# A hybrid SSM and attention block: four q/k slabs go into Strassen pairs, and the SSM projection's products move

## The chip, the cores and the metric

The kernel runs on one core of a Trainium2 chip. A core has five engines that run their own instruction streams side by side: TensorE (PE; its weight loads are listed as PEld), VectorE (DVE), ScalarE (ACT), GpSimd (POOL) and SyncE (SP). In this kernel SP issues every DMA. Work in progress lies in SBUF and, for matmul results, in PSUM (eight banks of 128 x 512 float32). What is measured is the device time of one execution in microseconds (us).

## The reference

One decoder layer with sequence length 1024 and model width 1024, in float32, for batch 1:

```python
h = _rmsnorm(x, norm_w) * (1.0 + scale[:, None, :]) + shift[:, None, :]
proj = jnp.einsum("bsd,de->bse", h, w_in)
z_ssm, xbc, dt_raw, q, k, v, z_att, f_logit, g_logit = jnp.split(proj, offsets, axis=-1)
y_ssm = _ssd_branch(z_ssm, xbc, dt_raw, ...)     # Mamba-2, 16 heads of 64, chunks of 128
y_att = _fox_branch(q, k, v, z_att, f_logit, b_f)   # causal attention, 8 heads of 128
g_ssm, g_att = jnp.split(jax.nn.sigmoid(g_logit + b_gate), N_BRANCHES, axis=-1)
merged = g_ssm * (y_ssm @ w_proj_ssm) + g_att * (y_att @ w_proj_att)
x = x + gate[:, None, :] * (merged @ w_out)
return _rmsnorm(x, final_norm_w)
```

(The last lines are written with @ for the einsum of the reference.) `scale`, `shift` and `gate` come from c. Nearly all of the work is in matrix products: the input projection to 8472 columns, the scores and the weighted sums of attention, and the three projections of 1024 x 1024 at the end.

## The kernel before

**Numbers.** Each float32 operand is split into a high part (cast to fp32r, on ACT) and a low part (the rest, by a subtraction on DVE); a product is high x high + high x low + low x high, so three matmuls for one. The helper `split` (L97 to L99) does this. Nearly all cast and subtraction rows in the profile are its lines L98 and L99, whatever they work on.

**Stages, in order.** (1) h is normalized, transposed and kept in SBUF as eight blocks `hh` and `hl` (pool `hpool`); 64 KB of each partition. (2) The slabs of the input projection. A slab is 128 output columns over all 1024 positions. A plain slab (`c_slab`) takes 2 x 8 x 3 = 48 matmuls of 128 x 128 x 512 (L111 to L113). Two slabs can be made together as a pair (`c_pair`) by the Strassen-Winograd scheme: seven products of 12 matmuls (L497 to L500), so 84 for two slabs, with four sums of weights, seven splits and three additions of results on DVE. The list `PAIRS` names 19 pairs, made one after the other in the pool `pa`; the tuple `WPREP` hangs the sums of later weights on some of them. Results that are needed later are written to DRAM. (3) The Mamba scan (pools `sd`), with the v slabs and seven plain q/k slabs (`SPILL`) put between its steps; these are written to DRAM. (4) Attention, by head. (5) The projections `ps` (SSM), `pa` (attention) and `o` (output), each a 1024 x 1024 x 1024 product by the same seven-product scheme on blocks of 512.

**Attention.** `attend(h, ...)` works through four groups qq = 3, 2, 1, 0 of two blocks of 128 queries: score matmuls (tile `lg`, L1030), the masked addition with row minimum on DVE (L1031), the exponential on ACT (L1036), the scaling on POOL (L1039), transposes on PE (tile `tp`, L1051), the split (`pth`, `ptl`, L1054 and L1055), and the weighted sum (tile `pv`, L1061), which DVE multiplies by the gate (L1064). A head's output is stored by L1065. `qk_slab(h + 1)` gets the next head's q and k: a slab in `SPILL` is loaded from DRAM and split as a whole (two operations of 1024 columns); any other is made there as a plain slab from `hh` and `hl`, with its result split out of PSUM. q and k of a head have two buffers each. In the kernel before, nine slabs are made this way: q1, k1, q2, q3, k3, q4, q5, q6, k7.

**What sets the order.** The program is traced in Python order, and a scheduler then orders each engine's instructions by readiness and priority. The attention heads get a higher priority (`high_priority(offset=APRI)`); the slabs and the early products are placed where the heads leave room. Tiles come from pools with a fixed number of buffers per tag; an instruction that needs a buffer waits until it is free. `issue_after(ins)` orders the instructions of its block on the engine of `ins` behind `ins`, on that engine alone.

**The SSM projection's products.** The scheme's products are numbered 1 to 7. Products 1 and 2 use unchanged blocks of the right operand; 6, 7 and 4 use forms that DVE makes by subtractions; 5 uses b11 after a subtraction; 3 uses b22. Some need results of others: 6 adds product 1's copy (x1), 7 is accumulated onto 6 (its copy is u3), 5 adds x1 or u2 and u3, 4 belongs onto u3, and 3 onto 5. When h's memory is closed (`hctx.close()`, at head `HCLOSE`), the pool `fin` takes its place, and with it eight buffers for forms (`bh`, `bl`), the copies and the blocks b12 and b22. `early(js)` loads pieces of the right operand (`us_scr`), makes the forms and runs the products of `js` in the three PSUM banks of the tile `mm`, while attention still runs. In the kernel before, products 1 and 2 are traced at head 6 and product 6 at head 7; 7, 5, 4 and 3 follow behind the heads, in the main part (`prod_c`), which opens five more PSUM banks and the tiles of the pool `frp` when attention's memory is free.

Lines that matter: L44 to L60 (the tables), `prod_c` L906 to L916, `early` L933 to L972, `qk_slab` L977, `attend` L1011, the head loop L1072 to L1088, the main part L1091 to L1118.

Of the kernel before, what the change touches and what calls it, by code (L numbers as in the profile page):

```python
# [31 lines left out]
P = 128  # L32
# [14 lines left out]
PSPILL = ()  # L47
SB = (3, 4, 3)
HCLOSE = 6
EARLY = {6: (1, 2), 7: (6,)}  # L50
# [15 lines left out]
def build(ctx, tc, t):  # L66
# [807 lines left out]
    def post(i, p, ps, x, held, done):  # L874

        if i == 1:
            x[p] = fin_tile("x1", 4)
            A.copy(out=x[p], in_=ps)  # L880
            held[1, p] = ps
        elif i == 6:
            V.tensor_tensor(out=ps, in0=ps, in1=x[p], op=ALU.add)
            A.copy(out=x[p], in_=ps)
            held[6, p] = ps
        elif i == 7:
            if (6, p) not in held:
                V.tensor_tensor(out=ps, in0=ps, in1=x[p], op=ALU.add)
                held[6, p] = ps
            held["u3", p] = fin_tile("u3", 4)  # L890
            A.copy(out=held["u3", p], in_=ps)
        elif i == 5:
            u3 = held.pop(("u3", p))
            V.tensor_tensor(out=u3, in0=ps, in1=u3, op=ALU.add)
            V.tensor_tensor(out=ps, in0=ps, in1=x[p], op=ALU.add)
            held[5, p] = ps
            done(1, 1, p, u3)
        else:
            done(*RESULT[i], p, ps)
# [31 lines left out]
    sx, held = {}, {}  # L931

    def early(js):  # L933
# [6 lines left out]
        def form(i):  # L940
            fs = []
            for k in range(4):
                if i == 2:
                    e = piece(4 + k, LO)
                else:
                    e = piece(k, LO)
                    for q in {1: (), 6: (12, 22)}[i]:
                        V.tensor_tensor(out=e, in0=ub[q][k], in1=e, op=ALU.subtract)
                fs.append(b_split(e))
# [8 lines left out]
        if js == (6,):  # L958
            for p in range(4):
                hi, lo = w_in("ps", 6, p)  # L960
                ps = bank()
                for k in range(4):
                    c = slice(k * P, (k + 1) * P)
                    PE.matmul(ps, lhsT=hi[:, c], rhs=fs[6][k][0], start=(k == 0), stop=False)
                    PE.matmul(ps, lhsT=hi[:, c], rhs=fs[6][k][1], start=False, stop=False)
                    PE.matmul(ps, lhsT=lo[:, c], rhs=fs[6][k][0], start=False, stop=(k == 3))
                V.tensor_tensor(out=sx[p], in0=ps, in1=sx[p], op=ALU.add)
            return
        for p in range(4):
            mine = {}  # L970
            for i in js:
                prod_c(i, "ps", fs[i], sx, mine, done, p)  # L972

    with tc.tile_pool(name="at", bufs=1, side="right") as at, \
# [36 lines left out]
        def attend(h, q, vhl, zg):  # L1011
# [5 lines left out]
            for qq in (3, 2, 1, 0):  # L1017
# [25 lines left out]
                for jp in range(qq + 1):  # L1043
# [12 lines left out]
                    for kb in (2 * jp, 2 * jp + 1):  # L1056
# [3 lines left out]
                        for i, (x, y) in enumerate(((vh, pth), (vl, pth), (vh, ptl))):  # L1060
                            PE.matmul(pv[:, o0:256], lhsT=x[kb // 4][:, kb % 4, vs], rhs=y[:, d:d + m],  # L1061
                                      start=(kb == 0 and i == 0), stop=(kb == 2 * qq + 1 and i == 2))
# [9 lines left out]
        for h in range(AH):  # L1072
# [14 lines left out]
            for _ in range(PREP[h]):  # L1087
                u_scaled(next(prep))  # L1088

# [5 lines left out]
    with tc.tile_pool(name="finp", bufs=1, space=PSUM) as fpp_:  # L1095
        fpp.append(fpp_)


        done_early = sum(EARLY.values(), ())
        b = {**ub, **b_quads(us_scr, (11, 21))}  # L1100
# [3 lines left out]
        prep_u = True  # L1104
        for i in ORDER:
            if i in done_early:
                continue
            if i in (5, 4) and prep_u:
                prep_u = False
                for p in range(4):  # L1110
                    t2 = tt_tile()
                    V.tensor_tensor(out=b[11][p], in0=b[12][p], in1=b[11][p], op=ALU.subtract)
                    V.tensor_tensor(out=t2, in0=b[22][p], in1=b[11][p], op=ALU.subtract)
                    V.tensor_tensor(out=b[21][p], in0=b[21][p], in1=t2, op=ALU.subtract)
            prod_c(i, "ps", b_form(i, b, lambda: raw_tile()[:, :512]), sx, held, ssm_done)
# [134 lines left out]
```

## Time and profile before

| | us |
|---|---|
| median of 3 runs | 1224.31 (1223.64 to 1227.98) |
| the profiled execution's own time | 1224.89 |
| its span, first to last instruction | 1223.2 |
| PE busy | 1162.6 |
| PE weight loads busy | 976.3 |
| DVE busy | 957.2 |
| ACT busy | 626.5 |
| POOL busy | 88.3 |

The profile is one execution on the chip. In its time line a row gives start, duration, engine, line of the program, operation, the tile written and those read, and in brackets the idle time before it with what ended it. In the table of stretches a row gives the stretch and its length, then for each engine the busy time and the number of instructions, then the granted clock of PE (1.00 is full), the mean busy share of the 16 DMA engines, and GB/s; such a table can also be asked for one tile alone. A matmul's end is modelled and matmuls overlap, so the busy time of PE is an upper bound of its work.

### The profile page before, as it was taken

How to read it: one execution, taken by the hardware profiler on the slowest of the kernel's cores; microseconds unless marked ns; L12 is line 12 of the kernel's file. 1: busy time of each engine (PE TensorE's matmuls, PEld its weight loads, DVE VectorE, ACT ScalarE, POOL GpSimd, SP SyncE). 2: the span in 40 equal slices, each digit the busy share in tenths (PEclk: the TensorE clock that was granted, in tenths of full speed). 3: DMA queues.
4: the chain of work that ended last, by engine and by line, in shares of the span. 5: the costliest groups of instructions: out<-in, count | busy, mean ns of one | idle time of the engine just before them, and what ended most of it. 6: DMA issues, size and time to landing. Idle time of an engine off the chain costs nothing.

```text
span 1223.2 us, 18391 instructions
## 1 busy us (share of the span) xinstructions
PE 1162.6 (95%) x6206; PEld 976.3 (80%) x6206; DVE 957.2 (78%) x1950; ACT 626.5 (51%) x1252; POOL 88.3 (7%) x152
## 2 busy tenths in 40 slices
PE   4899999999999999999999989999989998999997
PEld 2788888788877878998987777888877886788876
DVE  6956689788987685589999986664677968989967
ACT  5554444453443334777676633454456644354465
POOL 2000000000000000000000002222322220000001
PEclk9899999999999999999999999999999999999999
DMA  8765543655485665646545658422255526965333
GB/s 351 274 233 184 185 154 93 231 189 189 129 309 167 224 224 200 202 152 223 187 150 186 199 213 294 155 92 73 87 176 195 182 77 239 326 190 182 104 96 147
DMA packets 109018, 228.26 MB, mean 187 GB/s; under 512 B 12362, under 2 KB 20220, under 8 KB 107900
## 3 DMA queue, kind: packets, MB, share of 16 engines
q1 hardware_dynamic: 108924, 227.09, 55.1%
q8 instruction: 49, 0.80, 0.3%
q14 instruction: 45, 0.37, 0.1%
HBM read 159.14 MB, written 67.90 MB: 186 GB/s over the span
## 4 chain that ended last, share of the span: by engine, by line
PE 66%; DVE 15%; DMA 12%; issue 4%; ACT 3%; POOL 1%; SPq 0%; DVEq 0%; POOLq 0%; ACTq 0%
PE pp L497 4%; PE pp L499 4%; PE pp L500 4%; PE pv L1061 4%; PE mm L497 3%; PE mm L499 3%; PE mm L112 3%; PE mm L500 3%; PE mm L113 3%; PE lg L1030 3%; PE mm L111 3%; DMA ab<-a_scr 3%; PE tp L1051 2%; PE mm L915 2%; PE mm L913 2%
## 5 line engine op out<-in xcount | busy, mean ns | idle before, releaser
L98 ACT CAST wh<-wr 128x512 fp32r<-128x512 f32 (+1 forms) x214 | 130.8, 619 | 171.7 <-DMA wr<-w_c 35.0
L99 DVE TENSOR_TENSOR wl<-wr,wh 128x512 fp32r<-128x512 f32 (+1 forms) x214 | 145.5, 686 | 44.9 <-ACT wh L98 44.6
L112 PE MATMUL mm<-hl,wh 128*128 128x512 f32 x288 | 116.4, 404 | 1.9 <-DVE hl L306 1.9
L111 PE MATMUL mm<-hh,wh 128*128 128x512 f32 x288 | 115.7, 406 | 0.1
L113 PE MATMUL mm<-hh,wl 128*128 128x512 f32 x288 | 115.1, 400 | 0.0
L136 PE MATMUL mm<-wh,hh 128*128 128x256 f32 (+1 forms) x256 | 73.8, 289 | 2.4 <-DVE tmp L348 2.4
L137 PE MATMUL mm<-wl,hh 128*128 128x256 f32 (+1 forms) x256 | 74.4, 292 | 0.0
L138 PE MATMUL mm<-wh,hl 128*128 128x256 f32 (+1 forms) x256 | 73.6, 288 | 0.0
L1036 ACT ACTIVATE pr<-pr,sm 128x1024 f32<-128x1024 f32 (+3 forms) x64 | 49.9, 780 | 44.8 <-DVE sm L1035 38.1
L1054 ACT CAST pth<-tp 128x512 fp32r<-128x512 f32 (+1 forms) x80 | 42.5, 542 | 53.5 <-PE tp L1051 43.7
L1031 DVE CUSTOM_DVE_ANT_0 pr<-lg,fb 128x512 f32<-128x512 f32 (+1 forms) x96 | 51.3, 551 | 18.7 <-PE lg L1030 13.2
L112 PEld LDWEIGHTS mm<-hl,wh 128*128 128x128 f32 x288 | 55.0, 191 | 13.2 <-DVE hl L306 3.3
L113 PEld LDWEIGHTS mm<-hh,wl 128*128 128x128 f32 x288 | 54.9, 191 | 10.3
L111 PEld LDWEIGHTS mm<-hh,wh 128*128 128x128 f32 x288 | 54.5, 191 | 10.5 <-ACT hh L305 0.7
L690 ACT ACTIVATE ab<-ab,acs 128x128 f32<-128x128 f32 x128 | 41.2, 391 | 37.7 <-DMA ab<-a_scr 34.1
L1055 DVE TENSOR_TENSOR ptl<-tp,pth 128x512 fp32r<-128x512 f32 (+1 forms) x80 | 49.9, 630 | 10.2 <-ACT pth L1054 9.8
L1039 POOL TENSOR_SCALAR pr<-pr,sm 128x1024 f32<-128x1024 f32 (+3 forms) x64 | 52.2, 816 | 78.2 <-DVE sm L1038 65.4
L98 ACT CAST sh<-sr 128x512 fp32r<-128x512 f32 x57 | 33.9, 619 | 42.3 <-DVE sr L479 31.3
L796 POOL TENSOR_TENSOR fl<-fl,mhalf 128x8 f32<-128x8 f32 x1 | 1.6, 1648 | 699.0 <-DVE fl L794 699.0
L136 PEld LDWEIGHTS mm<-wh,hh 128*128 128x128 f32 x256 | 48.8, 191 | 2.8 <-DVE tmp L348 2.6
L138 PEld LDWEIGHTS mm<-wh,hl 128*128 128x128 f32 x256 | 49.1, 192 | 0.0
L137 PEld LDWEIGHTS mm<-wl,hh 128*128 128x128 f32 x256 | 48.9, 191 | 0.2
(406 smaller groups left out, 3485.5 us busy)
## 6 DMA issues: line engine op xcount, KB each, us to landing
wr<-w_c SPq DMA_DIRECT2D x116, 256.0 KB, 3.7
wa<-w_ada SPq DMA_DIRECT2D x8, 1024.0 KB, 11.4
g_scr<-gt SPq DMA_DIRECT2D x16, 512.0 KB, 4.2
ab<-a_scr SPq DMA_DIRECT2D x32, 256.0 KB, 3.9
gt<-g_scr SPq DMA_DIRECT2D x32, 256.0 KB, 4.0
wr<-w_ps SPq DMA_DIRECT2D x28, 256.0 KB, 2.7
wr<-w_pa SPq DMA_DIRECT2D x28, 256.0 KB, 2.7
wr<-so SPq DMA_DIRECT2D x28, 256.0 KB, 2.7
```

Of the source, the lines that this page charges most:

```text
L98: A.copy(out=hi[:, :n], in_=raw[:, :n])
L99: eng.tensor_tensor(out=lo[:, :n], in0=raw[:, :n], in1=f32(hi[:, :n]), op=ALU.subtract)
L111: PE.matmul(ps, lhsT=hi[:, cs], rhs=xh[k][:, hs], start=(k == 0), stop=False)
L112: PE.matmul(ps, lhsT=hi[:, cs], rhs=xl[k][:, hs], start=False, stop=False)
L113: PE.matmul(ps, lhsT=lo[:, cs], rhs=xh[k][:, hs], start=False, stop=(k == 7))
L136: PE.matmul(o, lhsT=xh[k][:, ts], rhs=hi[:, cs], start=(k == 0), stop=False)
L137: PE.matmul(o, lhsT=xh[k][:, ts], rhs=lo[:, cs], start=False, stop=False)
L138: PE.matmul(o, lhsT=xl[k][:, ts], rhs=hi[:, cs], start=False, stop=(k == 7))
L497: PE.matmul(ps, lhsT=f[0][:, w], rhs=xh[:, hs], start=(first and k == 0), stop=False, skip_group_check=True)
L499: PE.matmul(ps, lhsT=f[0][:, w], rhs=xl[:, hs], start=False, stop=False, skip_group_check=True)
L500: PE.matmul(ps, lhsT=f[1][:, w], rhs=xh[:, hs], start=False, stop=(k == 3), skip_group_check=True)
L1039: G.tensor_scalar(out=pr[:, :n], in0=pr[:, :n], scalar1=sm[:, 1:2], scalar2=0.5, op0=ALU.mult, op1=ALU.mult)
```

## The change

Four of the nine plain slabs that are made during attention (q4, q5, q6 and k7) are made as two Strassen pairs, (q4, q5) and (q6, k7), ahead of the last two pairs of gates in the pair stage. They are written to DRAM and loaded by `qk_slab` like those of `SPILL`. The last slab made from h is then k3, and h's memory is closed at head 3 (6 before). Products 1 and 2 are traced at head 3 (6 before), products 6 and 7 together at head 5 (6 at head 7, 7 in the main part before). Product 4 is traced behind the head loop, its matmuls on PE ordered behind the last matmul of the last head's weighted sum (`pv`); it used the open bank of product 6 before and gets a bank of its own now, with u3 added by DVE. Its form is made from pieces again (three subtractions for each block). The main part keeps products 5 and 3, and loads b11 alone (b11 and b21 before). The special form of `early` for product 6 alone is gone. The results of products 2 and 4 wait in DRAM (`m_scr`) until the main part loads them; before, it was product 2's alone.

```diff
--- before.py
+++ after.py
@@ -44,10 +44,10 @@
 Z0, XB0, Q0, K0, ZA0, G0 = 0, 8, 18, 26, 34, 42
 FIRST = (G0, G0 + 1, G0 + 2)
 SPILL = (("q", 0), ("k", 0), ("k", 2), ("k", 4), ("q", 7), ("k", 5), ("k", 6), )
-PSPILL = ()
+PSPILL = (("q", 4), ("q", 5), ("q", 6), ("k", 7))
 SB = (3, 4, 3)
-HCLOSE = 6
-EARLY = {6: (1, 2), 7: (6,)}
+HCLOSE = 3
+EARLY = {3: (1, 2), 5: (6, 7)}
 ORDER = (1, 2, 6, 7, 5, 4, 3)
 WPREP = {1: [('ps', 0)], 2: [('ps', 1)], 3: [('ps', 2)], 6: [('ps', 3), ('pa', 0)], 8: [('pa', 1)], 10: [('pa', 2), ('g', 0)], 12: [('pa', 3), ('g', 2), ('g', 3)], 11: [('g', 1)], 13: [('G', 0)], 15: [('o', 0)], 16: [('o', 1)], 17: [('o', 2)], 18: [('o', 3)]}
 PREP = (6, 1, 0, 0, 0, 0, 0, 0, 1)
@@ -896,6 +896,8 @@
             held[5, p] = ps
             done(1, 1, p, u3)
         else:
+            if i == 4 and (6, p) not in held:
+                V.tensor_tensor(out=ps, in0=ps, in1=held["u3", p], op=ALU.add)
             done(*RESULT[i], p, ps)
 
     def prod_bank(i, p, held):
@@ -928,7 +930,7 @@
         SP.dma_start(out=gt, in_=g_scr[j][:, HI if tk else LO])
         return gt
 
-    sx, held = {}, {}
+    sx, held, last_mm = {}, {}, {}
 
     def early(js):
 
@@ -942,10 +944,16 @@
             for k in range(4):
                 if i == 2:
                     e = piece(4 + k, LO)
+                elif i == 7:
+                    e = raw_tile()[:, :512]
+                    V.tensor_tensor(out=e, in0=ub[22][k], in1=ub[12][k], op=ALU.subtract)
                 else:
                     e = piece(k, LO)
-                    for q in {1: (), 6: (12, 22)}[i]:
+                    for q in {1: (), 6: (12, 22), 4: (12, 22)}[i]:
                         V.tensor_tensor(out=e, in0=ub[q][k], in1=e, op=ALU.subtract)
+                    if i == 4:
+                        e2 = piece(4 + k, LO)
+                        V.tensor_tensor(out=e, in0=e2, in1=e, op=ALU.subtract)
                 fs.append(b_split(e))
             return fs
 
@@ -955,21 +963,12 @@
             m_scr[ch, tk, p] = dram.tile([P, 512], F32, name=f"m_scr{ch}{tk}{p}")
             SP.dma_start(out=m_scr[ch, tk, p], in_=gt)
         fs = {i: form(i) for i in js}
-        if js == (6,):
-            for p in range(4):
-                hi, lo = w_in("ps", 6, p)
-                ps = bank()
-                for k in range(4):
-                    c = slice(k * P, (k + 1) * P)
-                    PE.matmul(ps, lhsT=hi[:, c], rhs=fs[6][k][0], start=(k == 0), stop=False)
-                    PE.matmul(ps, lhsT=hi[:, c], rhs=fs[6][k][1], start=False, stop=False)
-                    PE.matmul(ps, lhsT=lo[:, c], rhs=fs[6][k][0], start=False, stop=(k == 3))
-                V.tensor_tensor(out=sx[p], in0=ps, in1=sx[p], op=ALU.add)
-            return
         for p in range(4):
-            mine = {}
+            mine = {("u3", p): held["u3", p]} if js == (4,) else {}
             for i in js:
                 prod_c(i, "ps", fs[i], sx, mine, done, p)
+            if 7 in js:
+                held["u3", p] = mine["u3", p]
 
     with tc.tile_pool(name="at", bufs=1, side="right") as at, \
             tc.tile_pool(name="atp", bufs=1, space=PSUM) as atp:
@@ -1058,8 +1057,9 @@
                         o0 = 128 if (last and kb % 2) else 0
                         m = 256 - o0
                         for i, (x, y) in enumerate(((vh, pth), (vl, pth), (vh, ptl))):
-                            PE.matmul(pv[:, o0:256], lhsT=x[kb // 4][:, kb % 4, vs], rhs=y[:, d:d + m],
-                                      start=(kb == 0 and i == 0), stop=(kb == 2 * qq + 1 and i == 2))
+                            last_mm["pv"] = PE.matmul(pv[:, o0:256], lhsT=x[kb // 4][:, kb % 4, vs],
+                                                      rhs=y[:, d:d + m], start=(kb == 0 and i == 0),
+                                                      stop=(kb == 2 * qq + 1 and i == 2))
                 o = zg[:, qq * 256:(qq + 1) * 256]
                 V.tensor_tensor(out=o, in0=pv[:, :256], in1=o, op=ALU.mult)
             SP.dma_start(out=o_scr[h], in_=zg[:, :S])
@@ -1086,6 +1086,8 @@
                     ub = b_quads(us_scr, (12, 22))
             for _ in range(PREP[h]):
                 u_scaled(next(prep))
+        with tc.issue_after(last_mm["pv"].ins):
+            early((4,))
 
 
     frp = rctx.enter_context(tc.tile_pool(name="frp", bufs=1, side="right"))
@@ -1096,23 +1098,15 @@
         fpp.append(fpp_)
 
 
-        done_early = sum(EARLY.values(), ())
-        b = {**ub, **b_quads(us_scr, (11, 21))}
+        b = {**ub, **b_quads(us_scr, (11,))}
+
         def ssm_done(ch, tk, p, ps):
             V.scalar_tensor_tensor(out=mq[11 + 10 * ch + tk][p], in0=g_in(p + 4 * ch, tk), scalar=1.0, in1=ps,
                                    op0=ALU.add, op1=ALU.mult)
-        prep_u = True
-        for i in ORDER:
-            if i in done_early:
-                continue
-            if i in (5, 4) and prep_u:
-                prep_u = False
-                for p in range(4):
-                    t2 = tt_tile()
-                    V.tensor_tensor(out=b[11][p], in0=b[12][p], in1=b[11][p], op=ALU.subtract)
-                    V.tensor_tensor(out=t2, in0=b[22][p], in1=b[11][p], op=ALU.subtract)
-                    V.tensor_tensor(out=b[21][p], in0=b[21][p], in1=t2, op=ALU.subtract)
-            prod_c(i, "ps", b_form(i, b, lambda: raw_tile()[:, :512]), sx, held, ssm_done)
+        for p in range(4):
+            V.tensor_tensor(out=b[11][p], in0=b[12][p], in1=b[11][p], op=ALU.subtract)
+        for i in (5, 3):
+            prod_c(i, "ps", b_form(i, b), sx, held, ssm_done)
 
         for ch, tk, p in m_scr:
             SP.dma_start(out=mq[11 + 10 * ch + tk][p], in_=m_scr[ch, tk, p])
```

## The prediction

> **What bounds the kernel now.** I read the page first, then the busy time by stage, then the time line and the chain of waits around the attention heads and behind them.
>
> ```profile
> span 1223.2 us, 18391 instructions
> ...
> PE 1162.6 (95%) x6206; PEld 976.3 (80%) x6206; DVE 957.2 (78%) x1950; ACT 626.5 (51%) x1252; POOL 88.3 (7%) x152
> ...
> PE   4899999999999999999999989999989998999997
> PEclk9899999999999999999999999999999999999999
> ```
>
> PE is the engine that sets the end nearly everywhere. But a matmul's end is modelled, so the row of nines hides short idle times. The step from one 512-column matmul to the next shows what one really costs:
>
> ```profile
> 1018.94 0.39 PE L915 MATMUL pp<-bh,wl 128*128 128x512 f32 x1
> 1019.17 0.39 PE L913 MATMUL pp<-bh,wh 128*128 128x512 f32 x1
> ...
> 1025.76 1.28 DVE L1112 TENSOR_TENSOR b<-b,b 128x512 f32<-128x512 f32 x2
> ```
>
> So 0.23 us per matmul, not 0.39, and for DVE 1.28 - 0.68 = 0.60 us per 512-column operation in a row, 0.68 alone. By stage (the pairs; attention from the end of k3's slab, where the change begins to differ; the two stretches behind attention):
>
> ```profile
> core 0: us, PE busy (x) PEld busy (x) DVE busy (x) ACT busy (x) POOL busy (x), PEclk, DMA share, GB/s
> 123.00:500.00 377.00, 372.44 (x1642) 301.71 (x1641) 295.02 (x457) 165.37 (x284) 0.00 (x0) 1.00 0.58 194
> ...
> 808.00:1018.40 210.40, 200.65 (x1178) 174.16 (x1176) 144.30 (x381) 108.59 (x221) 56.02 (x94) 0.98 0.38 124
> 1018.40:1060.00 41.60, 38.83 (x162) 29.96 (x163) 37.98 (x63) 18.08 (x32) 0.00 (x0) 1.00 0.95 337
> 1060.00:1136.00 76.00, 76.00 (x330) 61.80 (x329) 68.32 (x113) 38.18 (x68) 0.00 (x0) 1.00 0.64 204
> ```
>
> In the pairs 377.0 / 1642 = 0.23: PE has no room. From 1060 on it is the same (76.0 / 330). Between 1018.4 and 1060, 162 x 0.23 = 37.3 of 41.6 us: 4.3 idle. In attention the q/k slabs and the early SSM products ("fillers" from here on; all of them write the tile mm) run in what the heads leave of PE. A head ends where its output is stored; the windows below are cut at these stores, and the PE count is the number of fillers in each.
>
> ```profile
> 887.34 0.32 SPq L1065 DMA_DIRECT2D o_scr<-zg  x1
> ...
> 1018.81 0.38 SPq L1065 DMA_DIRECT2D o_scr<-zg  x1
> ```
>
> ```profile
> 808.00:819.70 11.70, 7.95 (x32) 5.40 (x30) 0.68 (x1) 0.58 (x1) 1.00 0.22 69
> 819.70:858.50 38.80, 22.59 (x89) 16.14 (x89) 1.28 (x2) 1.11 (x2) 1.00 0.25 88
> 858.50:887.30 28.80, 12.18 (x48) 8.73 (x48) 1.36 (x2) 1.09 (x2) 1.00 0.28 92
> 887.30:917.00 29.70, 6.37 (x24) 4.29 (x24) 1.36 (x2) 1.09 (x2) 0.99 0.52 176
> 917.00:960.10 43.10, 21.46 (x84) 15.19 (x84) 3.39 (x5) 3.42 (x6) 0.93 0.55 178
> 960.10:998.30 38.20, 24.09 (x96) 17.67 (x96) 5.51 (x8) 1.77 (x3) 1.00 0.47 146
> 998.30:1018.80 20.50, 0.00 (x0) 0.00 (x0) 0.00 (x0) 0.00 (x0) 1.00 0.12 40
> ```
>
> Take the fillers' 0.23 us each off, and a head costs net: rest of head 1: 11.7 - 7.4 = 4.3; head 2: 18.3; head 3: 17.8; head 4: 24.2; head 5: 23.8; head 6: 16.1; head 7: 20.5. Together 125.0 and 373 x 0.23 = 85.8 of fillers: 210.8. Heads 2, 3 and 6 have fillers enough and PE is full. Head 4 runs out of them, head 5 begins where h's memory turns into the memory of the early products, and head 7 has none. What the turn of the memory costs shows in the time line, the windows and the chain of waits:
>
> ```profile
> 915.89 0.69 DVE L99 TENSOR_TENSOR bl<-wr,bh 128x512 fp32r<-128x512 f32 x1 [1.42 <-ACT bh L98]
> ...
> 918.25 0.80 PE L1030 MATMUL lg<-kh,qh 128*128 128x512 f32 x1 [3.17 <-DVE sm L1031]
> ```
>
> ```profile
> 914.90:918.20 3.30, 0.18 (x2) 0.03 (x1) 2.31 (x7) 2.53 (x5) 0.00 (x0) 0.71 1.06 406
> 918.20:922.20 4.00, 3.95 (x14) 3.53 (x14) 2.06 (x8) 3.02 (x7) 3.85 (x4) 0.50 1.00 354
> ```
>
> ```profile
> 909.50 5.72 DMA wr<-us_scr
> ...
> 930.24 2.44 DMA wr<-us_scr
> ```
>
> The forms of products 1 and 2 stand in DVE's queue, wait for ACT's cast and that for a piece landing 5.7 us after its issue; the head's own DVE work stands behind them, PE waits 3.2 us, and in the windows the granted clock is 0.50 for the next 4.0 us, another 2.0 lost.
>
> **The change, part by part.** *Four slabs (q4, q5, q6, k7) leave attention:* 4 x 48 matmuls, 192 x 0.23 = 44.2 us of fillers. *Two pairs come into the pair stage:* 2 x 84 = 168 matmuls; PE is full there, so all of it lies on the path: +38.6. Their DVE work (14 operations of 0.60, 8.4 us in a pair of 19.3) hides beside PE, since DVE has 82 us free of 377; with that cover gone it would be up to 17. *Four more stores and four reloads* of 512 KB go through SP's queue. The stores lie in the pair stage (DMA share 0.58), the reloads in attention (0.38): nothing by themselves. A reloaded slab also needs a split:
>
> ```profile
> L99 DVE TENSOR_TENSOR kl<-qt,kh 128x1024 fp32r<-128x1024 f32 x4 | 4.9, 1218 | 1.8 <-ACT kh L98 1.8
> ```
>
> 1.2 us on DVE in place of four operations of 0.60 (two of the weights, two of the result). *Product 7 moves into head 5's early call, product 4 behind the last pv matmul.* Attention before held 96 + 48 + 36 of products 1, 2, 6 and 7; the 12 left of product 7 ran behind it. After, it holds 192: products 1, 2, 6, 7. So attention from 808 loses 373 - 192 = 181 fillers, 41.6 us. DVE there: -16 x 0.60 (slabs) + 4.9 (reloads) - 1.8 (three adds of product 7 that accumulating in one bank saves) + 12 (16 form operations of product 4 and its four weight halves, which the order on PE doesn't hold back) = +5.5: 150 us.
>
> *h's memory is freed at head 3.* The last slab that reads h is then k3, done at 808, not k7 at 907. The turn described above comes 100 us earlier, and the SSM's forms with it: 8 + 4 piece loads, then 8 for product 4, on SP behind the reloads.
>
> What do the heads cost with 192 fillers? Those run as soon as they are ready, so I let heads 2 and 3 be filled (18.3 and 17.8, as now) and the rest to be short. For an unfilled head the trace gives 17.8 from below (a filled one: all its waits covered) and 24.2 from above (head 4, half filled and without cover in its second half); head 7, the only one with none at all, took 20.5, which includes an end behind which nothing follows. I take 20.0 for heads 4 to 6, 20.5 for head 7. For the turn: heads 4 and 5 were 24.2 + 23.8 - 2 x 17.8 = 12.4 over filled ones; half of it I put to want of fillers, half, 6.2, to the turn (its bounds: 0, if the waiting heads 2 and 3 cover it, and 12.4). Sum: 4.3 + 18.3 + 17.8 + 60.0 + 20.5 + 6.2 + 44.2 = 171.3, against 210.8: -39.5.
>
> *The passage.* Behind attention PE had 12 matmuls of product 7, and then waited for b11's load, DVE's subtraction, ACT's cast:
>
> ```profile
> 1020.56 0.69 DVE L1112 TENSOR_TENSOR b<-b,b 128x512 f32<-128x512 f32 x1 [2.24 <-DMA b<-us_scr]
> ...
> 1022.03 1.19 PE L913 MATMUL pp<-bh,wh 128*128 128x512 f32 x4 [0.62 <-ACT bh L98]
> ```
>
> After, product 4 gives 48 matmuls, 11.0 us, in the three mm banks that stay open, and b11 can land meanwhile. The order that holds them behind the last pv matmul holds nothing else: what stands behind them on PE are products 5 and 3, which need b11 and the memory of attention anyway. Behind attention are 48 x 3 = 144 matmuls of the SSM, not 156: -2.8. Of the 4.3 us idle I take 2.7 back (bounds: 0 and 4.3), as DVE loses eight subtractions there and gains four adds (product 4 needs product 7's sum): -5.5 in all. b21's four loads go where DMA is full (0.95); four more reloads of finished parts come when it has eased (0.64 from 1060 on): nothing.
>
> Total: 38.6 - 39.5 - 5.5 = -6.4. The profiled execution took 1224.9 (1.7 outside its span), so 1218.5; the runs' median is 0.6 lower: **1217.9, said as 1218.0**. It is about what 24 matmuls cost (5.5): the idle time stays nearly what it was.
>
> [...]
>
> **The rivals.**
> (a) *The heads stay covered.* The early products spread over heads 3 to 7, and each costs 17.8: 4 x 17.8 = 71.2 in place of 80.5, so -9.3: 1208.6. For it: heads 2, 3 and 6 were full with 48 to 96 fillers, and 192 over five heads are 38 each. Against: only eight operand tiles exist for forms, and fillers run when they can.
> (b) *Attention starves, slower than before.* The fillers are gone by head 4 and heads 4 to 7 each cost what head 4 did: 4 x 24.2 = 96.8, so +16.3: 1234. The gain is gone from 80.5 / 4 + 6.4 / 4 = 21.7 us a head on. For it: DVE rises from 144 of 210 us to 150 of 171, and sits in every head's chain. Against: head 7.
> (c) *Product 4 comes late.* Its forms are not ready at the last pv matmul: a piece's landing (2.4 to 5.7), three subtractions, a cast and a split (3.0) lie open, about 7, the half clock costs 2.0 more, and the 2.7 are not won: +11.7, 1229.6.
> (d) *Half clock in the heads.* Two idle stretches like that at 914.9 in each of heads 4 to 7: 17.8 + 2 x (3.3 + 2.0) = 28.4 a head, +33: 1251. Against: head 7 had a clock of 1.00. [...]
> That the change doesn't do what it says (early products that start no sooner) would leave the 192 fillers to later heads; that is (a).
>
> **How the numbers follow.** The forecast, with its own range 1212 to 1226, gets 0.54; (a) 0.18, (b) 0.14, (c) 0.10, (d) 0.04. 0.5% is 6.1 us, about what a measurement of this kernel can tell from no change: faster is below 1218.2, slower above 1230.4. A little over half of the forecast's chance is faster: 0.28, with (a) 0.46. Slower are (b), (d) and a little of (c): 0.19. The rest is 0.35. For the range I go down to 1206, below (a), and up to 1235, just above (b); (d) and the ends are left out.
>
> **What would show it.** Right, if heads 4 to 7 end some 20 us apart with few mm matmuls between them, k3's slab is followed by a wait of lg for DVE with a clock drop, the pairs' stretch is some 39 us longer, and PE runs 48 matmuls behind the last pv without a wait. Wrong, if heads 4 to 7 come 24 us apart or wait over 3 us at a time, if the first matmul of product 4 is late by some us, or if the pair stage grows by clearly more than 39.

## The result, and the profile after

The changed kernel takes 1241.25 us (median of 4 runs, 1237.6 to 1241.98) against 1225.32 for the kernel before: ratio 1.0113, 95% interval 1.0093 to 1.0132. It is slower by 16 us where 6 less were forecast, and lies above the range that was given (1206 to 1235).

The page of the changed kernel:

```profile
span 1239.6 us, 18407 instructions
...
PE 1169.2 (94%) x6182; PEld 978.4 (79%) x6182; DVE 975.5 (79%) x1970; ACT 638.9 (52%) x1272; POOL 90.8 (7%) x152
...
PE   4899999999999999999999997998988989999997
...
PEclk9899999999999999999999998998999999999999
```

24 matmuls fewer, and 16.4 us more of span. Where they lie is read from the stages. The two profiles first differ in the pairs; what lies between them and k3's slab, the scan and the first head, is the same to within 1.5 us; attention is compared from the end of k3's slab (808.4 before, 848.9 after). The stages of the changed kernel, columns as in the prediction (pairs, attention from k3's slab, everything behind attention):

```profile
114.00:530.00 416.00, 411.83 (x1786) 332.86 (x1785) 312.10 (x485) 175.08 (x306) 0.00 (x0) 1.00 0.56 188
...
848.90:1041.00 192.10, 171.54 (x1001) 145.10 (x1000) 152.21 (x387) 110.81 (x223) 59.01 (x94) 0.96 0.46 154
...
1041.00:1239.60 198.60, 188.82 (x813) 151.95 (x811) 170.09 (x291) 101.56 (x191) 4.69 (x8) 0.99 0.61 202
```

and the same two stages of the kernel before that the prediction did not show in these bounds:

```profile
115.00:491.00 376.00, 371.44 (x1605) 299.47 (x1604) 293.52 (x457) 159.52 (x278) 0.00 (x0) 1.00 0.58 195
...
1018.80:1223.20 204.40, 193.08 (x828) 154.59 (x826) 176.04 (x301) 104.20 (x197) 4.69 (x8) 0.99 0.58 192
```

| | before | after | difference | predicted |
|---|---|---|---|---|
| up to the end of k3's slab | 808.4 | 848.9 | +40.5 | +38.6 |
| attention from there | 210.4 | 192.1 | -18.3 | -39.5 |
| behind attention | 204.4 | 198.6 | -5.8 | -5.5 |

Two of the three terms came as worked out: the pairs (376 to 416) and the passage. The whole miss is in attention. The table of fillers, cut at the heads' stores (the tile mm alone, PE's count is the number of fillers), for the changed kernel:

```profile
848.90:858.10 9.20, 0.00 (x0) 0.00 (x0) 0.68 (x1) 0.57 (x1) 0.91 0.83 265
858.10:907.50 49.40, 25.22 (x96) 17.54 (x96) 2.04 (x3) 2.34 (x4) 0.88 0.51 173
907.50:954.80 47.30, 24.52 (x96) 17.42 (x96) 3.44 (x5) 4.66 (x8) 1.00 0.66 214
954.80:977.00 22.20, 0.00 (x0) 0.00 (x0) 0.00 (x0) 0.00 (x0) 0.92 0.46 162
977.00:1000.50 23.50, 0.00 (x0) 0.00 (x0) 0.00 (x0) 0.00 (x0) 1.00 0.42 139
1000.50:1021.10 20.60, 0.00 (x0) 0.00 (x0) 0.00 (x0) 0.00 (x0) 1.00 0.10 39
1021.10:1041.00 19.90, 1.09 (x5) 0.98 (x6) 0.00 (x0) 0.00 (x0) 1.00 0.12 40
```

Net of fillers at 0.23 us, as in the prediction: the rest of head 1 took 9.2, head 2 27.3, head 3 25.2, heads 4 to 7 22.2, 23.5, 20.6 and 18.7. All 192 fillers ran in heads 2 and 3, and these two cost more beside their fillers than a head with none. What held head 2 up is seen at the turn of the memory, first in the chain of waits, then in ACT's and PE's time lines:

```profile
851.66 7.06 DMA wr<-us_scr
```

```profile
851.82 1.16 ACT L1035 ACTIVATE pr<-pr,sm 128x1024 f32<-128x1024 f32 x1
...
855.30 0.38 PE L1060 MATMUL pv<-ptl,vh 128*128 128x256 f32 x1 [0.49 <-DVE ptl L1054]
...
858.74 0.62 ACT L98 CAST bh<-wr 128x512 fp32r<-128x512 f32 x1 [5.68 <-DMA wr<-us_scr]
859.27 1.04 ACT L98 CAST vh<-vt 128x1024 fp32r<-128x1024 f32 x1
...
860.75 0.80 PE L1029 MATMUL lg<-kh,qh 128*128 128x512 f32 x1 [2.84 <-DVE sm L1030]
```

A cast for a form of product 1 or 2 stands in ACT's queue and waits 5.68 us for its piece; behind it stand the split of the next v block and the exponentials of head 2. And the clock falls:

```profile
853.00:856.40 3.40, 2.38 (x12) 1.63 (x12) 3.40 (x10) 0.06 (x1) 1.60 (x2) 1.00 0.96 313
856.40:870.10 13.70, 10.38 (x37) 8.14 (x36) 9.28 (x22) 8.65 (x17) 4.84 (x6) 0.50 0.96 340
```

13.7 us at a clock of 0.50, in which PE was busy for 10.4. In this stretch a 512-column matmul starts 0.43 us after the one before it (861.34 and 861.77), at 1.00 just ahead of it 0.22 (852.56 and 852.78). By an estimate from these numbers about half of the 10.4, 5 us, would have been saved at full clock if nothing else had held it.

### The profile page after: what moved, and what is told of

It reads as the page before. It is cut to its first block, busy times and chain, and to the rows that moved or that the text cites. A ratio compares the mean times of both kernels' runs of the same rounds, so it can differ in the third digit from the quotient of the medians.

```text
span 1239.6 us, 18407 instructions
## 1 busy us (share of the span) xinstructions
PE 1169.2 (94%) x6182; PEld 978.4 (79%) x6182; DVE 975.5 (79%) x1970; ACT 638.9 (52%) x1272; POOL 90.8 (7%) x152
## 4 chain that ended last, share of the span: by engine, by line
PE 62%; DVE 17%; DMA 12%; issue 4%; ACT 3%; SPq 1%; POOL 0%; DVEq 0%; POOLq 0%; ACTq 0%
PE pp L497 5%; PE pp L499 5%; PE pp L500 5%; PE mm L497 3%; PE mm L499 3%; PE mm L500 3%; PE pv L1060 3%; DMA ab<-a_scr 2%; PE lg L1029 2%; DMA wr<-w_c 2%; PE mm L112 2%; PE mm L111 2%; PE mm L113 2%; PE pp L915 2%; PE pp L917 2%
## 5 line engine op out<-in xcount | busy, mean ns | idle before, releaser
L112 PE MATMUL mm<-hl,wh 128*128 128x512 f32 x224 | 91.7, 409 | 2.2 <-DVE hl L306 2.2
L113 PE MATMUL mm<-hh,wl 128*128 128x512 f32 x224 | 90.5, 405 | 0.0
L111 PE MATMUL mm<-hh,wh 128*128 128x512 f32 x224 | 89.7, 407 | 0.1
L98 ACT CAST sh<-sr 128x512 fp32r<-128x512 f32 x63 | 37.7, 619 | 50.0 <-DVE sr L479 34.5
L915 PE MATMUL mm<-bh,wh 128*128 128x512 f32 x128 | 51.9, 405 | 3.5 <-ACT wh L98 3.2
L1060 PE MATMUL pv<-pth,vh 128*128 128x256 f32 (+1 forms) x160 | 46.6, 291 | 7.0 <-DVE zg L1064 3.3
L112 PEld LDWEIGHTS mm<-hl,wh 128*128 128x128 f32 x224 | 43.3, 193 | 11.5 <-DVE hl L306 3.3
L1060 PE MATMUL pv<-ptl,vh 128*128 128x256 f32 (+1 forms) x160 | 48.6, 304 | 2.8 <-DVE ptl L1054 2.6
L916 PE MATMUL mm<-bl,wh 128*128 128x512 f32 x128 | 50.7, 396 | 0.0
```

The costliest lines, as they stand in the source:

```text
L98: A.copy(out=hi[:, :n], in_=raw[:, :n])
L111: PE.matmul(ps, lhsT=hi[:, cs], rhs=xh[k][:, hs], start=(k == 0), stop=False)
L112: PE.matmul(ps, lhsT=hi[:, cs], rhs=xl[k][:, hs], start=False, stop=False)
L113: PE.matmul(ps, lhsT=lo[:, cs], rhs=xh[k][:, hs], start=False, stop=(k == 7))
L915: PE.matmul(ps, lhsT=hi[:, c], rhs=bf[k][0], start=(new and k == 0), stop=False, skip_group_check=True)
L1060: last_mm["pv"] = PE.matmul(pv[:, o0:256], lhsT=x[kb // 4][:, kb % 4, vs], rhs=y[:, d:d + m], start=(kb == 0 and i == 0), stop=(kb == 2 * ...
```

## The experiments

The first theory, **F** (feeding): the early products' loads, casts and splits hold the heads up in the in-order queues. Its rival, **S** (starvation): the loss is in heads without fillers. The times of each kernel stand beside those of the kernel before on the same chip, which took 1225.4 to 1226.3 in these comparisons.

### The slabs alone

```diff
-PSPILL = ()
+PSPILL = (("q", 4), ("q", 5), ("q", 6), ("k", 7))
```

> The kernel before with one part of the change: q4, q5, q6 and k7 as two pairs. h's memory still closes at head 6, products 1, 2 and 6 stay early at heads 6 and 7, 7, 5, 4, 3 behind attention. The pairs add about 39.6 us to the pair stage in any case. Theory F (feeding: the early products' piece loads, casts and splits stand in the in-order queues of ACT and DVE ahead of the heads' own work, and that cost heads 2 and 3 some 17 us in the changed kernel; a head without fillers costs about 20.5): attention loses the 44.2 us of the four slabs and pays a few us for heads without fillers, no second crowd of forms; about 1222 us. Theory S (starvation: a head without fillers costs 24 or more, and that is where the loss is): heads 3 to 5 are without fillers here, attention loses only some 30 us; about 1234 us.

Measured: 1236.1 us, ratio 1.0076 (1.0051 to 1.0100). S was nearer in time. From the first score matmul to the end of head 7 attention took 259.9 us against 289.7: it lost 29.8 us with 192 matmuls that cost 44.2 elsewhere. Heads 3 and 4, now without fillers, in the table of the tile mm:

```profile
897.30:919.10 21.80, 0.00 (x0) 0.00 (x0) 0.00 (x0) 0.00 (x0) 1.00 0.44 145
919.10:942.60 23.50, 0.00 (x0) 0.00 (x0) 0.00 (x0) 0.00 (x0) 1.00 0.39 136
```

So taking the four slabs out of attention gives back 14.4 us less than their matmuls, 3.6 a slab, which is more than the 24 matmuls saved (5.5). The move of the slabs loses by itself. But this run doesn't part S from F as it was meant to. The early products are traced at head 6 here, yet the scheduler ran the first of them as soon as k3's slab was done. Head 2 in the table of the tile mm:

```profile
856.50:897.30 40.80, 18.89 (x72) 12.88 (x72) 0.00 (x0) 1.75 (x3) 0.91 0.54 180
```

All 72 fillers there are matmuls of early products, and the head took 24.2 net, against 18.3 in the kernel before, with the clock at 0.91. The turn of the memory had moved here as well. So the 14.4 us hold both cover that was lost and an earlier turn; the light filler below measures cover alone.

### The moves alone

```diff
-EARLY = {6: (1, 2), 7: (6,)}
+EARLY = {6: (1, 2), 7: (6, 7)}     # product 4 behind the last pv, as in the change; slabs and HCLOSE as before
```

> The other part alone: all nine slabs plain in attention as before, h's memory closed at head 6, products 1 and 2 at head 6, 6 and 7 together at head 7, product 4 behind the last pv matmul, 5 and 3 in the main part. Theory S: heads are filled as before and the passage wins its 5.5 us: about 1220 us. Theory F: the same turn of the memory as in the kernel before, with four more forms to feed before the end of attention: the passage wins 5.5, the feeding takes back 0 to 5: 1220 to 1225 us. Over 1228 would say that the moves themselves cost, wherever they stand.

Measured: 1227.2 us, ratio 1.0014 (0.9999 to 1.0030): not to be told from no change. The time behind attention fell from 204.4 to 197.4, and attention grew from 289.7 to 298.9. Some 18 matmuls more ran in attention, about 4 of these 9.2 us; the rest goes to feeding one more product's forms and product 4's (head 6 took 20.7 net, 16.1 before). Together they take back what the passage wins. With the slabs' 10 us, about 4 of the 16 are left for what tracing the early products at heads 3 and 5 adds; the turn of the memory behind k3's slab is already in the 10.

### No early product

```diff
-HCLOSE = 6
-EARLY = {6: (1, 2), 7: (6,)}
+HCLOSE = 3
+EARLY = {}                         # with the pairs; all seven products behind attention
```

> The slabs as pairs, h's memory closed at head 3, but no early product: attention from k3 on holds no filler and no forms at all; products 1, 2, 6, 7, 5, 4, 3 all run behind it. It measures a head without fillers and without feeding. Theory F: heads 2 to 7 come about 20.5 us apart, attention from k3 takes some 133 us in place of 192, 44.2 us of matmuls come in behind, with some 5 of waits in the passage: about 1231 us, faster than the changed kernel. Theory S: heads 2 to 7 come 24 us or more apart and the 44.2 us come on top: 1250 us or more.

Measured: 1238.7 us, ratio 1.0095 (1.0063 to 1.0127): between the two. Heads 3, 4 and 6, without fillers and without anything to feed:

```profile
878.70:902.50 23.80, 0.00 (x0) 0.00 (x0) 0.00 (x0) 0.00 (x0) 1.00 0.40 132
902.50:925.80 23.30, 0.00 (x0) 0.00 (x0) 0.00 (x0) 0.00 (x0) 1.00 0.41 138
...
949.50:970.20 20.70, 0.00 (x0) 0.00 (x0) 0.00 (x0) 0.00 (x0) 1.00 0.10 40
```

This is the clean price of a head without fillers: 23 to 24 us in heads 2 to 5, 20 to 21 in heads 6 and 7, where no more k, q and v are loaded and split for a next head (the DMA share falls from 0.40 to 0.10). And attention from k3's slab took 141.4 us with no early product, 192.1 with 192 matmuls of them: 50.7 us for 44.2 us of matmuls. The early products filled nothing; they cost more in attention than their own time. Behind attention they cost 247.0 - 198.6 = 48.4.

### The blocks b12 and b22 later

```diff
-                early(EARLY[h])
-                if 1 in EARLY[h]:
+                if 6 in EARLY[h]:
                     ub = b_quads(us_scr, (12, 22))
+                early(EARLY[h])
```

> The changed kernel with one edit: the eight loads of b12 and b22 (2 MB), which SP issued just ahead of the pieces of products 1 and 2 at the turn of the memory, are traced at head 5, right ahead of products 6 and 7. In the changed kernel a piece landed 7.06 us after its issue, and ACT's cast that waited for it held the exponentials back. Theory F: the pieces land in about 3 us and 4 to 6 us of head 2 come back: about 1236 us. Theory S: no change, 1241 us.

Measured: 1238.0 us, ratio 1.0092 (1.0064 to 1.0119). That is 3 us less than the changed kernel, but the intervals overlap, and the landing that was to shrink did not. In the chain of waits, with the loads of the blocks (L922) still ahead of the piece:

```profile
847.64 0.43 SPq L922
...
848.11 0.43 SPq L922
...
848.64 6.95 DMA wr<-us_scr
```

The edit changed the order of tracing, but not what ran: SP issued the eight loads at the turn all the same (845.9 to 851.9), between the pieces as in the changed kernel (848.9 to 854.9). So this run doesn't show whether these loads make the pieces late; that stays open.

### A light filler, and the same with DVE work

```diff
+            if h >= HCLOSE:         # on the kernel with no early product
+                with tc.issue_after(gate):        # the last pv matmul of the head before
+                    for p in range(4):
+                        ps = mm_tile()
+                        for k in range(12):
+                            PE.matmul(ps, lhsT=xw[:, :P], rhs=xw, start=(k == 0), stop=(k == 11))
+                        A.copy(out=xj[:, 8 * p:8 * p + 8], in_=ps[:, :8])      # e5
+                        V.tensor_tensor(out=xj, in0=ps, in1=f32(xw), op=ALU.add)   # e6: 3 or 4 of these instead
```

> The kernel without early products (e3_no_early, 1238.7 us, whose heads 3 to 7 took 23.8, 23.3, 23.7, 20.7 and 20.0 us with no filler) with 48 matmuls of 512 columns added in each of heads 3 to 7, from constant tiles that are always there, ordered on PE behind the last pv matmul of the head before; their sums are used for nothing. 240 matmuls, 55 us of PE. They need nothing of DVE and 0.2 us of ACT each dozen: a filler as light as can be. Theory C (cover: a head has about 5.5 us of waits that a filler fits into): heads of about 29 us, as heads 3 had in the kernel before with a plain slab; +33 us, 1272 us. Theory N (fillers only add, and the waits stay): heads of 32 to 35 us, +55 us, 1294 us.

> The same added matmuls, but DVE reads each dozen's sum three or four times in operations of 512 columns, 13 a head or 7.8 us of DVE, about what an early SSM product needs of it for its 48 matmuls (10 to 16), where a plain slab needs 4. Again used for nothing. Theory D (the early products are bad fillers because of their DVE work, which stands in the heads' chain): the cover is lost, heads of 33 us and more, 1290 us or more. If it was the waits for pieces and weights alone: as with the light filler, about 1272 to 1276 us.

Measured: 1276.5 us (ratio 1.0422, 1.0402 to 1.0442) for the light filler and 1282.0 (1.0456, 1.0431 to 1.0481) for the one with DVE work. Head 4 in both, all tiles, light above and heavy in the second fence:

```profile
910.40:941.00 30.60, 29.45 (x180) 25.78 (x179) 18.25 (x51) 15.08 (x34) 8.00 (x15) 1.00 0.32 106
```

```profile
912.80:944.50 31.70, 30.00 (x180) 25.82 (x179) 25.85 (x64) 14.40 (x30) 8.00 (x15) 1.00 0.32 102
```

The light filler adds 37.8 us for 55.2 us of matmuls: 17 us, some 3.5 a head, went into idle time. Cover is real, as theory C had it, though somewhat smaller. The 39 us of added DVE work cost 5.5 us, about 1 a head, and theory D, which wanted 18 and more, falls: it is not the amount of DVE work that makes an early product a bad filler.

### Products 6 and 7 spread

```diff
-EARLY = {3: (1, 2), 5: (6, 7)}
+EARLY = {3: (1, 2), 4: (6, 7)}     # and early((6, 7)) inside issue_after(last pv matmul of head 4)
```

> The changed kernel with products 6 and 7 traced at head 4 and their matmuls ordered on PE behind head 4's last pv matmul, so that they run in heads 5 to 7 and not in head 3; their forms may still be made before. Theory C: the 96 matmuls find waits in heads 5 and 6 (5.5 and 3 us) and head 3 loses its crowd: 8 to 10 us come back, 1232 us. Theory N: the time only moves, 1241 us.

Measured: 1241.8 us, ratio 1.0132 (1.0116 to 1.0149): nothing came back. Head 3, now without fillers, and head 5 with most of products 6 and 7 (tile mm):

```profile
905.70:935.40 29.70, 0.00 (x0) 0.00 (x0) 0.67 (x1) 0.00 (x0) 0.83 0.68 225
...
959.20:1002.10 42.90, 22.71 (x90) 16.09 (x89) 2.77 (x4) 4.66 (x8) 1.00 0.51 166
```

Head 3 took 29.7 us with no filler at all, 6 more than without early products: only forms and weights were prepared in it, at a clock of 0.83. And head 5, with 90 fillers, took 22.2 net. This points away from the matmuls and where they stand, to what comes with them.

### k6 the other way

```diff
-SPILL = (("q", 0), ("k", 0), ("k", 2), ("k", 4), ("q", 7), ("k", 5), ("k", 6), )
+SPILL = (("q", 0), ("k", 0), ("k", 2), ("k", 4), ("q", 7), ("k", 5), )   # and FILL without the entry for k6
```

> The kernel before with one edit the other way: k6, which it made as a plain slab between the steps of the Mamba scan and stored, is made in attention instead, one more light filler of 11 us there and 11 less in the scan. Theory C: the four slabs that left attention took only 29.8 us with them (7.5 each), so k6 costs about 7.5 there; if the scan is full of PE work it gives 11 back: 1222 us. If the scan has waits of its own that k6 covered, it gives back less: 1226 us or more.

Measured: 1230.1 us, ratio 1.0037 (1.0023 to 1.0051): slower. The scan with k6 (kernel before) and without it:

```profile
491.00:729.00 238.00, 228.51 (x1696) 205.23 (x1694) 207.32 (x495) 160.22 (x386) 1.65 (x1) 1.00 0.57 184
```

```profile
492.00:730.00 238.00, 219.15 (x1650) 198.93 (x1648) 204.72 (x491) 157.55 (x381) 1.65 (x1) 0.97 0.55 179
```

46 matmuls fewer in the profile and the same 238.0 us: leaving the slab out of the scan gained nothing, with the granted clock at 0.97 there and not at 1.00. In attention it cost 5.4 (295.1 against 289.7).

### Early products without loads

```diff
-            e = raw_tile()[:, :512]
-            SP.dma_start(out=e, in_=us_scr[j][:, hs])
-            return e
+            return rb[:, :512]                              # e9: no piece is loaded
...
-            hi, lo = w_in(n, i, p)
+            hi, lo = split(rb, hi_tile(), lo_tile(), 512)   # e10: nor a weight, for the early products
```

> The changed kernel with the loads of the early products' pieces left out: products 1, 2, 6, 7 and 4 take a resident tile in their place, so the output is not the reference's; every cast, subtraction, weight load and matmul stays (one subtraction writes to another buffer). In the changed kernel heads 2 and 3 took 27.3 and 25.2 us beside their fillers, against 22.8 and 23.8 with no early products and about 20 with a light filler. Theory W (the waits for pieces in the queues of ACT and DVE make the difference): heads 2 and 3 lose some 4 us each, and 8 to 10 us come back: 1232 us. If it is the work of the forms itself, or the lump of 96 matmuls a head: 1239 to 1241 us.

> The same, and the weights of the early products come from the resident tile too: no load of any kind in front of their casts and splits (the loads of the gates and of b12 and b22 stay). Output not the reference's. Theory W: another 2 to 5 us, as a weight's load landed 5.3 us after its issue in head 3 and ACT's cast stood on it: 1229 us. If the weights are early enough anyway: as without pieces.

Measured: 1235.5 us without the pieces (ratio 1.0073, 1.0052 to 1.0094) and 1227.3 without pieces and weights (1.0005, 0.9990 to 1.0019). Leaving out these 40 loads (20 pieces, 20 weights) gives back 13.9 of the 16 us; every cast, split and matmul is still there. Attention of the last kernel from k3's slab, all tiles:

```profile
846.60:1025.00 178.40, 165.31 (x1003) 140.15 (x1002) 150.64 (x385) 108.97 (x220) 57.32 (x94) 1.00 0.34 113
```

The clock stays at 1.00, and 178.4 is 13.7 less than 192.1: the gain lies in this stage. Theory W, the waits for loads, holds. Without the pieces alone, heads 1 and 2 came down to 18.4 and 20.1 net, but head 3 still took 26.7; without the weights too it took 20.5. The kernel before has such waits at its own turn, and no run leaves the loads out of it. So the 13.9 us are what the loads cost the changed kernel; how much of it is a difference between the two kernels is not shown.

### The kernel before with the blocks later

> The kernel before with the one edit that gave the changed kernel 3 us: the eight loads of b12 and b22 are traced right ahead of product 6 and not behind products 1 and 2, so that the pieces don't stand behind them at the turn of the memory. Theory W: the turn costs 2 to 4 us less: 1222 us. If product 6 then waits for the blocks: 1225 us or more.

The edit is that of the blocks above, made in the kernel before. Measured: 1225.2 us, ratio 0.9993 (0.9976 to 1.0009): no change, and heads 4 and 5 cost 23.5 and 23.9 net (24.2 and 23.8 before). Here too SP issued the eight loads where it had, from 908.8 to 915.1 (907.7 to 914.9 before), so what they cost at the turn stays untested.

### Light matmuls in two lumps

```diff
-            if h >= HCLOSE:
+            if h in (3, 4):
...
-                    for p in range(4):
+                    for p in range(8):
```

> The kernel without early products with 96 light matmuls (constant operands, sums unused) in each of heads 3 and 4 and none later: 192, 44.2 us, in lumps as the changed kernel has them, but with nothing to feed. With 48 a head the light filler left 20.5, 19.3, 20.5, 17.4 and 18.2 us of head beside it, against 23.8, 23.3, 23.7, 20.7 and 20.0 without. Theory C: a head has room for some 4 to 6 us of filler and no more, so the two lumps save 8 to 12: 1238.7 + 44.2 - 10 = 1273 us, 34 us for 192 matmuls where the changed kernel's cost 50.7. If lumping is harmless, as much is saved as by 48 in five heads, 16 us: 1267 us.

Measured: 1272.9 us, ratio 1.0382 (1.0359 to 1.0405): 34 us for 192 matmuls, as theory C had it. The two heads (tile mm):

```profile
878.50:918.20 39.70, 23.10 (x93) 16.69 (x93) 0.00 (x0) 1.33 (x8) 1.00 0.25 80
918.20:958.00 39.80, 23.30 (x95) 16.84 (x93) 0.00 (x0) 1.34 (x8) 1.00 0.24 80
```

18.3 and 18.0 us net by these counts. So 96 fillers in a head do cover its waits, down to nearly what a filled head took before (17.8), when nothing has to be fed. So the changed kernel's 27.3 and 25.2 don't come from the lump alone.

### Own buffers for the pieces, and k7 in the scan

Why do the loads come late? In SP's time line of the changed kernel, pieces (L939) and the first weight of product 1 (L85):

```profile
782.95 0.45 SPq L939 DMA_DIRECT2D wr<-us_scr  x1
...
795.93 0.32 SPq L939 DMA_DIRECT2D wr<-us_scr  x1
...
851.66 0.38 SPq L939 DMA_DIRECT2D wr<-us_scr  x1
...
860.11 0.34 SPq L85 DMA_DIRECT2D wr<-w_ps  x1
```

Four pieces are issued from 783 to 796 and fill the four raw buffers; nothing can be done with them until h's memory is free, 50 us later. Only then do the other pieces get a buffer, and the weights after those. The kernel before does the same at its later turn: four pieces from 810.2 to 843.8, the first weight at 916.6.

```diff
         def piece(j, hs, tag=None):
-            e = raw_tile()[:, :512]
+            e = raw_tile()[:, :512] if tag is None else fin_tile(tag, 4)   # "x1", "u3" for products 1 and 2
```

```diff
-SPILL = (("q", 0), ("k", 0), ("k", 2), ("k", 4), ("q", 7), ("k", 5), ("k", 6), )
+SPILL = (("q", 0), ("k", 0), ("k", 2), ("k", 4), ("q", 7), ("k", 5), ("k", 6), ("k", 7))   # on the kernel before; and FILL with an entry for k7
```

> The changed kernel with the eight pieces of products 1 and 2 loaded into the buffers of x1 and u3, which lie idle until those products end, and not into the four raw buffers that the weights use as well. Same output. In the changed kernel four pieces took all four raw buffers at 783 to 796 us and held them until 850; the other four pieces were issued from 851.7, the first weight of product 1 at 860.1. Theory R (the shared raw buffers are why the loads come late): weights are there before the turn, all pieces are issued at once; heads 1 and 2 lose 5 to 8 us of waits: 1235 us. Theory B (the transfers themselves are slow, as DMA is 0.83 busy at the turn): 1239 to 1242 us.

> The kernel before with k7 made between the steps of the Mamba scan and stored, like k6, and not in attention: the last slab that reads h is then q6, and the turn of the memory comes some 7 us of work earlier. Without k6 the scan took as long as with it (238.0 us in both profiles, 48 matmuls fewer). Theory C: the scan still has room, k7 costs 0 to 5 us there, attention loses about 7.5 and the turn starves as before: 1219 to 1224 us. If k6 had filled the last of its room: k7 costs 11 there, 1228 us or more.

Measured: own buffers 1235.1 us (ratio 1.0078, 1.0057 to 1.0099), 6 less than the changed kernel with the same loads, though the two intervals just meet. It is what theory R forecast for products 1 and 2. Its SP line now has the first weight at

```profile
780.00 0.34 SPq L85 DMA_DIRECT2D wr<-w_ps  x1
```

and heads 1 and 2 took 18.8 and 19.3 net in place of 22.2 and 27.3. Head 3 took 26.6: products 6, 7 and 4 still use the shared buffers. That these are the same thing once more was not tried by itself. The edit also changed the order at the turn: the pieces were issued first (849.4 to 853.8) and the loads of b12 and b22 behind them. How much of the gain is due to the weights' early loads and how much to this order is not separated.

k7 in the scan: 1219.9 us, ratio 0.9959 (0.9939 to 0.9979), the one kernel here that is faster than both. The end of head 0 came 4.9 us later than in the kernel before (794.5 against 789.6), with k7's 48 matmuls more up to there; from there to the end of head 7 it took 219.4 us in place of 229.2. So this slab cost 4.9 us in the scan and had cost 9.8 in attention; in the pairs a slab costs 10 (40.0 us for four).

## Why the prediction was wrong, step by step

**The pairs, +38.6.** Right: +40.5 at the end of k3's slab, +40.0 in the stage alone. DVE's added work stayed hidden, as said.

**The slabs leave attention, -41.6 of fillers.** Right as a count: 192 fillers ran where there had been 373 (and 5 of product 4).

**"I let heads 2 and 3 be filled (18.3 and 17.8, as now)", with 6.2 for the turn.** This step failed. With the rest of head 1 it made 4.3 + 18.3 + 17.8 + 6.2 = 46.6; measured were 9.2 + 27.3 + 25.2 = 61.7. These 15.1 us are most of the 20.8 by which attention missed (192.1 against 171.3). The prediction counted an early product as the same filler as a slab, by its matmuls. The kernel without their loads shows what stood in its place: attention took 178.4, so 13.7 us go with the loads of pieces and weights, where the sum had 6.2 for the whole turn. The prediction had one such wait in its own rows (a piece landing after 5.7 us, PE waiting 3.2, the clock at 0.50) and priced it once, at half of what it could be; the loads of products 6, 7 and 4 had no term. It didn't ask which buffers these loads need. They share four raw buffers with the weights, and when h's memory is freed the pieces hold all of them. Why the loads come late is shown in part only: giving products 1 and 2 other buffers brought 6 us back, with the order of the loads changed too.

**"I take 20.0 for heads 4 to 6."** Too low, a size and not a mechanism: 22.2, 23.5 and 20.6 came, 6.3 us more in all. The kernel with no early product has the clean figures, 23.3 and 23.7 for heads 4 and 5. The row it was set by, head 7, has no v, q and k to load and split for a next head, and the bound from above, 24.2, was the better one for heads 2 to 5.

**The passage, -5.5.** Right: -5.8. Product 4's matmuls ran right behind the last pv. But the moves alone show that the matmuls moved ahead and the forms of products 7 and 4 together took about as much back in attention as the passage won; the sum had the forms at +5.5 us of DVE work and no time.

**"It is about what 24 matmuls cost: the idle time stays nearly what it was."** This is what fell as a whole. Even without the early products' loads the kernel only breaks even (1.0005), against a kernel before that still has its own: heads 4 to 7, without fillers, took 22.3, 23.7, 20.6 and 18.7 net there too. The idle time that the slabs had covered comes open.

**The rivals.** (b) named the right side and came nearest to the time, with 1234, but put all of it on heads 4 to 7 at 24.2 each; they took 85.0, not 96.8. The point from which it decides, 21.7 us a head, was about reached (21.3), and the larger part came from heads 2 and 3. (c) did not happen. (d) neither: the clock fell twice, not in each head: to 0.50 at the turn (856.4 to 870.1) and as head 4 began (955.4 to 958.8). (a) was refuted.

**"PE waits 3.2 us, and in the windows the granted clock is 0.50 for the next 4.0 us."** This was read too coarsely: the clock fell during the wait, not behind it. In the prediction's row from 914.9 to 918.2 the mean clock is 0.71, so by an estimate from that row it fell from 1.00 to 0.50 some 1.4 us after the row began, at about 916.3; from 916.4 to 923.1 it was 0.50. The 3.4 us up to 916.3, in the kernel before:

```profile
912.90:916.30 3.40, 2.09 (x11) 1.33 (x10) 1.98 (x6) 1.01 (x2) 1.42 (x2) 1.00 0.97 324
```

PE was busy for 2.09 of them, at 1.00. The sum doesn't rest on this reading.

## What to carry to other kernels

Work that runs in another stage's idle time costs there only what is over its cover: price it where it stands (one slab here: 10 us in the full pair stage, 5.4 to 9.8 between attention heads, nothing to 4.9 in the scan), not by its instructions. Two fillers with the same matmuls are not the same filler; look at what each needs loaded and which shared buffers its loads take, because an operand fetched early into a common ring can keep everything else's operands out until it is used. Loads that can't be used yet should not hold buffers that others need. And an edit of the order of tracing tests an order of issue only if the trace shows that the order changed.

## What the runs showed of the hardware that was not expected

The clock of TensorE fell without a long idle time before it. The prediction's rows had it at 0.50 beside a wait of 3.2 us. In the changed kernel, from 853.0 to 856.4, PE was busy for 2.38 of 3.4 us by the profile, and no idle time in it was longer than half a microsecond (0.49 in the row shown); in the kernel before it was busy for 2.09 us from 912.9 to 916.3, and idle from 915.1 on. The clock in the changed kernel then stayed at 0.50 for 13.7 us. That holds the wait of 2.84 us, but from its end at 860.75 it took 9.3 us more, with PE busy for 8.9 of them. What makes the clock fall, and what brings it back, is not shown by these runs. The price of 2.0 us that the prediction gave to a half clock was too low for such a stretch: about 5 us by the estimate above.

The other is how little DVE's load mattered: 39 us of added DVE operations in five heads whose PE work stayed the same (in head 4 DVE was busy for 25.85 us against 18.25) cost 5.5 us.
